# Sixteen pairs in place of twelve in the sum-of-products form of a down projection, and four buffers for its split activations

## The chip, the core and the metric

The kernel runs on one core of a Trainium2 chip. The metric is device time in microseconds of one launch, from all inputs in device memory to the output in device memory. The engines named below are TensorE (PE in the profile; its weight loads are PEld), VectorE (DVE), ScalarE (ACT), GpSimd (POOL) and SyncE (SP, which issues most transfers here). They run their own instruction queues, each in its order, and hand work to each other through semaphores.

## What is computed

The kernel is one decoder layer: token mixers, cross-attention and a gated feed-forward block, for 256 tokens of width 2048. Only the last step of the last block is touched:

```python
def conv_glu_ffn(h, w_up, conv_w, conv_b, w_down):     # h: 256 x 2048
    u = h @ w_up                                       # 256 x 16384
    uc = conv_b + sum(conv_w[j] * shift_right(u, CONV_WIDTH - 1 - j) for j in range(CONV_WIDTH))
    gate, up = split_cols(uc, (D_FF, D_FF))            # D_FF = 8192
    return (jax.nn.gelu(gate, approximate=True) * up) @ w_down   # the down projection: 8192 x 2048

x = x + rms_norm(conv_glu_ffn(h, ffn_w_up, ffn_conv_w, ffn_conv_b, ffn_w_down), ffn_post_norm)
```

All of it is float32. TensorE multiplies rounded operands (float32r), so each operand is split into a rounded part and a rest (hi and lo), and a product is three matmuls: hi by hi, lo by hi, hi by lo.

## The kernel before

**The down projection.** Its output of 256 tokens by 2048 columns is made in two blocks of 1024 columns (`fd`, L2060 to L2063). A block runs over 64 chunks; a chunk is one k tile, 128 rows of `w_down` by 1024 columns, 512 KB. A block holds four PSUM banks (`tm`): token half 0 or 1 by column half 0 or 1, each 128x512. A plain chunk is 4 banks times 3 matmuls, 12 matmuls of 128x512; the activations are the stationary operand, the weights the moving one.

**Feeding a chunk.** SP loads the raw weights (`raw`, four buffers); ACT rounds them into `wh` (five buffers, L448), DVE subtracts for `wl` (L520). When the program stands at chunk i it has written the splits up to chunk i+3 and the loads up to chunk i+7. The activations of two chunks at a time are split by `asplit` (L1911): ACT copies to `as`, DVE subtracts. There are two `as` buffers, and at each even chunk the split for two chunks later is written.

**Pairs.** In each block some neighbouring pairs of chunks, listed in `SEVEN` (L1906), go another way. The pair is a product of 2x2 blocks: the activations as token half by k tile, the weights as k tile by column half (`b11`, `b12` from the first chunk, `b21`, `b22` from the second). It is done with seven block products of sums instead of eight block products, so 7 x 3 = 21 matmuls in place of 24 (`seven_products`, L532). `prepare` (L452) makes the sums in steps, one for each chunk that passes (`ahead_of_pairs`, L492): sums of weights go into `t`, sums of activations into `f` (all inside the tile `end`, which is one buffer for all of them), and their splits into `ts`, `t4` and `sa`. The raw weights of a pair go into the single buffer `sraw`, also in `end`; one of its blocks is overwritten by a sum before it is split. Four of the seven products add up in four further banks (`more`); `join_sums` (L556) adds those together after the last pair of the block, and the evacuation (`fd_evac`) adds the result to the block's own banks.

**What sets the order.** The program order is written by Python loops: `work` (L577) walks over the chunks, and at every chunk calls, in turn, the splits (`lo`), the activations' split, the pair's loads (`pair_loads`, L481), further loads (`dma`), and one step of each pair's preparation that is due. A queue executes in that order, so that an instruction that waits holds all that stand behind it on its engine. Side work such as evacuations is spread by budgets (`Spread`).

Of the kernel before, what the change touches and what calls it, by code (L numbers as in the profile page):

```python
# [10 lines left out]
F32R = mybir.dt.float32r  # L11
# [4 lines left out]
P = 128  # L16
# [138 lines left out]
def _layer(ctx, tc, nc, d, dbg):  # L155
# [12 lines left out]
    def T2(name, shape=None, dt=F32):  # L168
        return mp.tile(shape or [P, 2, S], dt, tag="T2", bufs=6, name=name)
# [221 lines left out]
    class Feed:  # L391
        def __init__(self):
            a, g = blocks[0]["srcs"], blocks[1]["srcs"]
            self.src = a[:LEAD] + [c for p in zip(a[LEAD:], g) for c in p] + g[len(a) - LEAD:]
            self.src += [s for b in blocks[2:] for s in b["srcs"]]
            n, self.pairs, self.preps = sum(len(b["srcs"]) for b in blocks[:2]), {}, []
            for b in blocks[2:]:
                if b["seven"]:
                    for k in b["seven"]["at"]:
                        self.pairs[n + k], self.pairs[n + k + 1] = 0, 1  # L400
                        self.preps.append([n + k - 6, self.prepare(n + k, k), n + k, []])
                n += len(b["srcs"])
            self.raw, self.st, self.nd, self.ns, self.nl, self.nop = {}, {}, 0, 0, 0, 0

        def dma(self, upto):
# [36 lines left out]
        def hi(self, upto):  # L442
            while self.ns <= min(upto, len(self.src) - 1):
                self.dma(self.ns)
                r = self.raw[self.ns]
                wh = self.staged("wh", r)
                for o, v in self.pieces(self.ns, wh, r):
                    nc.scalar.copy(o, v)  # L448
                self.st[self.ns] = [wh, None]
                self.ns += 1  # L450

        def prepare(self, c, k):  # L452

            raw, t, f = M["sraw"], M["sums"], M["f4"]
            (b11, b12), (b21, b22) = ([raw[:, i, j * 512:j * 512 + 512] for j in range(2)] for i in range(2))
            x = acpair(k).rearrange("p k (t s) -> p (k t) s", t=2)
            dve.tensor_add(t[:, 0:512], b22, b12)
            dve.tensor_sub(f[:, 0:2], x[:, 1:2].broadcast_to((P, 2, P)), x[:, 0:4:3])
            yield
            dve.tensor_sub(b12, b12, b11)  # L460
            dve.tensor_sub(f[:, 2], x[:, 0], f[:, 1])
            dve.tensor_sub(f[:, 3], x[:, 2], f[:, 2])
            yield
            dve.tensor_add(t[:, 512:1024], b22, b12)
            sa = [T2("sa", [P, 4, P], F32R) for _ in range(2)]
            M["sa"].append(sa)
            act.copy(sa[0], f)
            yield
            dve.tensor_sub(t[:, 1024:], b21, t[:, 512:1024])
            dve.tensor_sub(sa[1], f, sa[0])  # L470
            ts, t4 = [C("ts", f"bg{j}", [P, 1024], F32R) for j in range(2)], [T2("t4", [P, 512], F32R) for _ in range(2)]
            M["ts"].append((ts, t4))
            act.copy(ts[0], t[:, 0:1024])
            yield
            dve.tensor_sub(ts[1], t[:, 0:1024], ts[0])
            act.copy(t4[0], t[:, 1024:])
            yield
            dve.tensor_sub(t4[1], t[:, 1024:], t4[0])
            yield

# [51 lines left out]
    def seven_products(b, banks, ci, w0h, w0l, w1h, w1l):  # L532
        sv = b["seven"]
        new = "more" not in sv
        if new:
            sv["ready"]()
            sv["more"] = [sv["pool"]("more") for _ in range(4)]
        (t, t4), a, sa = M["ts"].pop(0), M["a4"].pop(0), M["sa"].pop(0)
        half = lambda w, c: [v[:, 0, c * 512:c * 512 + 512] for v in w]
        tops = lambda c: [v[:, c * 512:c * 512 + 512] for v in t]  # L540
        old, more = banks, sv["more"]
        for n, (o, x, w) in enumerate(((more[0], [v[:, 0] for v in a], half((w0h, w0l), 0)),
                                       (old[0], [v[:, 2] for v in a], half((w1h, w1l), 0)),
                                       (more[2], [v[:, 1] for v in sa], half((w0h, w0l), 1)),
                                       (old[1], [v[:, 3] for v in sa], half((w1h, w1l), 1)),
                                       (more[3], [v[:, 0] for v in sa], tops(0)),
                                       (more[1], [v[:, 2] for v in sa], tops(1)),
                                       (old[2], [v[:, 3] for v in a], t4))):
            wh, wl = (turns(v) for v in w)
            mm(o, x[0], wh, start=new and o in more, stop=False)  # L550
            mm(o, x[1], wh, start=False, stop=False)
            mm(o, x[0], wl, start=False, stop=ci == sv["at"][-1] and o in more)
            if n in (1, 3, 5):
                side.half()

    def join_sums(sv):  # L556

        more, s = sv["more"], [M["join"][:, i] for i in range(4)]
        sv["sums"] = s
        act.copy(s[0], more[0])  # L560
        dve.tensor_add(s[2], s[0], more[1])
        yield
        dve.tensor_add(s[1], s[2], more[2])
        dve.tensor_add(s[2], s[2], more[3])
        yield
        dve.tensor_add(s[3], s[1], more[3])
        yield

    def run():
# [1333 lines left out]
        fu = block("fm", W("w_fw", f - 6), fu_xs(f), fw_evac(f), cols=256, wide=lambda k: M["fx"][:, :, k])  # L1903

    M["as"], M["a4"], M["sa"], M["ts"] = {}, [], [], []
    SEVEN = [12, 20, 30, 38, 48, 56], [10, 18, 28, 36, 46, 54]  # L1906

    def acpair(e):
        return M["ac"][e // 16][:, e % 16:e % 16 + 2] if e < 32 else M["ac"][2 + (e - 32) // 8][:, e % 8:e % 8 + 2]
# [1 line left out]
    def asplit(k):  # L1911

        if k not in M["as"]:
            n, e = k // 2, k % 64
            actile(e + 1)
            a = mp.tile([P, 1024], F32R, tag=f"au{n % 2}", bufs=1, name="as")
            a = a.rearrange("p (i j s) -> p i j s", i=2, j=2)
            split(a[:, 0], a[:, 1], acpair(e))
            for j in range(2):
                M["as"][k + j] = (a[:, 0, j], a[:, 1, j])  # L1920
            if e in SEVEN[k // 64]:
                M["a4"].append([a[:, i].rearrange("p k (t s) -> p (k t) s", t=2) for i in range(2)])
        return M["as"][k]
# [36 lines left out]
    def room():  # L1960
        end = mp.tile([P, 2 * KD * S], F32, tag="hT", bufs=1, name="end")
        M["gain"], M["sums"], M["f4"] = end[:, 0:2048], end[:, 2048:3584], end[:, 3584:4096].rearrange("p (k s) -> p k s", k=4)
        M["join"] = end[:, 4096:6144].rearrange("p (i c) -> p i c", i=4)
        M["sraw"] = end[:, 6144:8192].rearrange("p (i c) -> p i c", i=2)

    def load_gain():
# [6 lines left out]
    def fd_evac(n):  # L1973

        def gen(ps):
            if n == 0:
                M["z3", 0] = U("z3", [P, 2, 1024])
            else:
                M["z3", 1] = big("z31", [P, 2, 1024])
            z = M["z3", n]  # L1980

# [78 lines left out]
    fd = []  # L2060
# [106 lines left out]
```

## Time and profile before

| | us |
|---|---|
| median of 3 runs | 1796.6 (1796.27 to 1796.67) |
| the profiled execution | 1796.5 |
| its span, first to last instruction | 1794.7 |
| PE busy | 1785.2 (99%) |
| DVE busy | 1395.6 (78%) |
| ACT busy | 1076.7 (60%) |
| granted clock of TensorE, mean | 0.999 of 2.4 GHz |

The profiled execution lies 0.1 us from the median, and 1.8 us of it are outside of the span. A row of the timeline gives the start of an instruction, its duration, and in brackets the idle time of the engine before it with the instruction that ended it. The duration reaches until the result is written, and the next instruction of the engine may start a little earlier. So what a run of instructions costs an engine is read from start to start.

### The profile page before, as it was taken

The numbers are of one execution on the slowest core, as the hardware profiler recorded it, in microseconds if no ns is written. First come the engines' busy times: TensorE is split into PE (matmuls) and PEld (weight loads), VectorE is DVE, ScalarE is ACT, GpSimd is POOL, SyncE is SP. The second block draws the span as 40 slices with busy tenths as digits, with TensorE's granted clock in tenths as the row PEclk, the third lists the DMA queues.
The fourth block names the chain that finished last, engine by engine and source line by source line (L and its number), as shares of the span: only waits on it lengthen the run. The fifth ranks groups of instructions, "written<-read, shape, count | busy, mean of one in ns | idle before, by whom it ended". The sixth has DMA issues, their size and how long they took to land.

```text
span 1794.7 us, 30098 instructions
## 1 busy us (share of the span) xinstructions
PE 1785.2 (99%) x11778; PEld 1629.7 (91%) x11778; DVE 1395.6 (78%) x2020; ACT 1076.7 (60%) x1616; POOL 28.9 (2%) x51
## 2 busy tenths in 40 slices
PE   9999999999999999999999999999999999999998
PEld 9999988888888999999999999999999998888887
DVE  7869995766665767778878777877777778888887
ACT  7576454654554666677566667666655655556554
POOL 0100000000100000000000000000000000000000
PEclk9999999999999999999999999999999999999999
DMA  8755564454556676656666666666666676767664
GB/s 283 206 170 186 164 190 146 125 180 144 200 188 211 227 243 186 190 150 197 208 203 198 203 209 192 199 206 204 199 200 209 192 229 213 227 186 227 209 209 129
DMA packets 99134, 351.59 MB, mean 196 GB/s; under 512 B 10896, under 2 KB 13968, under 8 KB 98864
## 3 DMA queue, kind: packets, MB, share of 16 engines
q1 hardware_dynamic: 97888, 347.38, 61.3%
q8 instruction: 92, 1.51, 0.3%
q0 software_dynamic: 384, 1.18, 0.2%
q10 hardware_dynamic: 720, 1.12, 0.2%
q14 instruction: 50, 0.41, 0.1%
HBM read 347.01 MB, written 2.10 MB: 195 GB/s over the span
## 4 chain that ended last, share of the span: by engine, by line
PE 99%; DVE 0%; DMA 0%; ACT 0%; issue 0%; SPq 0%; DVEq 0%; ACTq 0%
PE fm L191 55%; PE tm L191 37%; PE more L191 2%; PE gram L191 0%; PE Y L191 0%; PE lv L191 0%; DMA op<-in_op_dram 0%; PE X L191 0%; PE num L191 0%; PE zwa L191 0%; PE U L191 0%; PE gramA L191 0%; PE xo L191 0%; PE zg L191 0%; PE Tn L191 0%; PE mT L1472 0%
## 5 line engine op out<-in xcount | busy, mean ns | idle before, releaser
L520 DVE TENSOR_TENSOR wl<-raw,wh 128x1024 fp32r<-128x1024 f32 (+1 forms) x617 | 741.5, 1218 | 128.6 <-ACT wh L448 125.9
L448 ACT CAST wh<-raw 128x1024 fp32r<-128x1024 f32 (+1 forms) x617 | 633.6, 1044 | 112.7 <-PE tm L191 61.7
L191 PE MATMUL fm<-fx,wh 128*128 128x512 f32 (+1 forms) x2240 | 672.8, 364 | 0.6 <-DVE fx L68 0.4
L191 PE MATMUL fm<-fx,wl 128*128 128x256 f32 x2048 | 558.3, 273 | 0.0
L191 PEld LDWEIGHTS fm<-fx,wh 128*128 128x128 f32 x2240 | 409.3, 190 | 49.9 <-DVE fx L68 1.0
L191 PEld LDWEIGHTS fm<-fx,wl 128*128 128x128 f32 x2048 | 393.3, 192 | 0.0
L191 PE MATMUL tm<-wh,as 128*128 128x512 f32 x856 | 254.8, 379 | 0.0
L191 PE MATMUL tm<-wh,hx 128*128 128x512 f32 (+1 forms) x832 | 243.9, 378 | 1.4 <-ACT hx L68 1.4
L191 PEld LDWEIGHTS tm<-wh,as 128*128 128x128 f32 x856 | 161.7, 189 | 23.2 <-DVE as L68 0.3
L68 ACT COPY ul<-fm 128x256 f32<-128x256 f32 x128 | 44.9, 373 | 225.5 <-PE fm L191 225.5
L191 PE MATMUL fm<-hx,wh 128*128 128x256 f32 x1024 | 174.5, 277 | 0.0
L191 PEld LDWEIGHTS tm<-wh,hx 128*128 128x128 f32 x832 | 151.0, 189 | 21.8 <-POOL wh L507 1.6
L191 PE MATMUL tm<-wl,as 128*128 128x512 f32 x428 | 162.2, 379 | 0.0
L191 PEld LDWEIGHTS fm<-hx,wh 128*128 128x128 f32 x1024 | 155.6, 192 | 1.1
L191 PE MATMUL tm<-wl,hx 128*128 128x512 f32 (+1 forms) x416 | 152.5, 373 | 0.4 <-DVE wl L520 0.3
L68 DVE TENSOR_TENSOR us<-fm,ul 128x256 f32<-128x256 f32 x128 | 48.5, 420 | 131.2 <-ACT ul L68 131.2
L191 PE MATMUL fm<-hx,wl 128*128 128x256 f32 x512 | 140.8, 275 | 0.0
L68 ACT CAST as<-ac 128x512 fp32r<-128x512 f32 x64 | 39.4, 617 | 118.8 <-PE tm L191 118.8
L191 PEld LDWEIGHTS fm<-hx,wl 128*128 128x128 f32 x512 | 98.3, 192 | 0.0
L191 PEld LDWEIGHTS tm<-wl,as 128*128 128x128 f32 x428 | 80.9, 189 | 11.5
L191 PEld LDWEIGHTS tm<-wl,hx 128*128 128x128 f32 x416 | 77.5, 189 | 11.2 <-DVE wl L520 0.5
L191 PE MATMUL fm<-mg,wh 128*128 128x512 f32 (+1 forms) x320 | 84.9, 340 | 0.0
(406 smaller groups left out, 2114.8 us busy)
## 6 DMA issues: line engine op xcount, KB each, us to landing
raw<-in_w_fw_dram SPq DMA_DIRECT2D x232, 512.0 KB, 4.3
raw<-in_w_in_dram SPq DMA_DIRECT2D x160, 512.0 KB, 3.7
raw<-in_w_fd_dram SPq DMA_DIRECT2D x104, 512.0 KB, 4.1
raw<-in_w_br_dram SPq DMA_DIRECT2D x32, 512.0 KB, 4.2
raw<-in_w_mw_dram SPq DMA_DIRECT2D x24, 512.0 KB, 4.8
raw<-in_w_fu_dram SPq DMA_DIRECT2D x24, 512.0 KB, 4.0
end<-in_w_fd_dram SPq DMA_DIRECT2D x24, 512.0 KB, 3.6
raw<-in_w_mo_dram SPq DMA_DIRECT2D x8, 512.0 KB, 4.1
```

What stands on the lines that cost most here:

```text
L68: return f(out, *a, **k)
L191: pe.matmul(out, lhsT, rhs, start=start, stop=stop, skip_group_check=True)
L448: nc.scalar.copy(o, v)
L520: nc.vector.tensor_sub(o, v, h)
```

## The change

- `SEVEN` lists eight pairs in each block where there were six. Most stand six chunks apart (four plain chunks between two pairs); before, the distances were eight and ten.
- `prepare` uses another set of seven products. Its first step makes two sums of weights in one 128x1024 instruction and a third in place of `b11`; it runs in four steps. A preparation starts five chunks ahead of its pair, or, where the pair ahead is six chunks away, as soon as that pair is past, four chunks ahead. Before it started six chunks ahead.
- `seven_products` takes the products in another order and into other banks; `join_sums` adds up accordingly, with one more copy on ACT.
- `asplit` has four buffers: the two of before and the two halves of a new tile `as2`. That tile takes the place in which the first block's result `z3` stood, which goes into `end`; `join` shares its place with the pair's sums, and so the second block's first preparation asks for the first block's evacuation to be written first.

```diff
-                        self.preps.append([n + k - 6, self.prepare(n + k, k), n + k, []])
+                        last = self.preps[-1][2] if self.preps else 0
+                        self.preps.append([max(n + k - 5, last + 2), self.prepare(n + k, k), n + k, []])
...
+            self.second = n - 64 + SEVEN[1][0]
...
+                assert self.pairs.get(self.ns) != 0 or self.ns in self.summed
...
-            raw, t, f = M["sraw"], M["sums"], M["f4"]
-            (b11, b12), (b21, b22) = ([raw[:, i, j * 512:j * 512 + 512] for j in range(2)] for i in range(2))
+            raw, t, f = M["sraw"].rearrange("p i (j n) -> p (i j) n", j=2), M["sums"], M["f4"]
             x = acpair(k).rearrange("p k (t s) -> p (k t) s", t=2)
-            dve.tensor_add(t[:, 0:512], b22, b12)
+            if c == self.second:
+                side.need(fd[0]["task"])
+            dve.tensor_add(t[:, 0:1024].rearrange("p (j n) -> p j n", j=2), raw[:, 0:1].broadcast_to((P, 2, 512)), raw[:, 1:3])
+            dve.tensor_add(raw[:, 0], t[:, 0:512], raw[:, 2])
+            self.summed.add(c)
+            yield
+            dve.tensor_add(t[:, 1024:], raw[:, 0], raw[:, 3])
             dve.tensor_sub(f[:, 0:2], x[:, 1:2].broadcast_to((P, 2, P)), x[:, 0:4:3])
-            yield
-            dve.tensor_sub(b12, b12, b11)
-            dve.tensor_sub(f[:, 2], x[:, 0], f[:, 1])
-            dve.tensor_sub(f[:, 3], x[:, 2], f[:, 2])
-            yield
-            dve.tensor_add(t[:, 512:1024], b22, b12)
-            sa = [T2("sa", [P, 4, P], F32R) for _ in range(2)]
-            M["sa"].append(sa)
-            act.copy(sa[0], f)
-            yield
-            dve.tensor_sub(t[:, 1024:], b21, t[:, 512:1024])
-            dve.tensor_sub(sa[1], f, sa[0])
             ts, t4 = [C("ts", f"bg{j}", [P, 1024], F32R) for j in range(2)], [T2("t4", [P, 512], F32R) for _ in range(2)]
             M["ts"].append((ts, t4))
             act.copy(ts[0], t[:, 0:1024])
             yield
+            dve.tensor_sub(f[:, 2], f[:, 1], x[:, 0])
+            dve.tensor_add(f[:, 3], x[:, 2], f[:, 2])
             dve.tensor_sub(ts[1], t[:, 0:1024], ts[0])
+            sa = [T2("sa", [P, 4, P], F32R) for _ in range(2)]
+            M["sa"].append(sa)
             act.copy(t4[0], t[:, 1024:])
-            yield
+            act.copy(sa[0], f)
+            yield
+            dve.tensor_sub(sa[1], f, sa[0])
             dve.tensor_sub(t4[1], t[:, 1024:], t4[0])
             yield
...
-        for n, (o, x, w) in enumerate(((more[0], [v[:, 0] for v in a], half((w0h, w0l), 0)),
-                                       (old[0], [v[:, 2] for v in a], half((w1h, w1l), 0)),
-                                       (more[2], [v[:, 1] for v in sa], half((w0h, w0l), 1)),
-                                       (old[1], [v[:, 3] for v in sa], half((w1h, w1l), 1)),
-                                       (more[3], [v[:, 0] for v in sa], tops(0)),
-                                       (more[1], [v[:, 2] for v in sa], tops(1)),
-                                       (old[2], [v[:, 3] for v in a], t4))):
+        for n, (o, x, w) in enumerate(((old[1], [v[:, 2] for v in a], half((w1h, w1l), 1)),
+                                       (more[0], [v[:, 0] for v in a], half((w0h, w0l), 1)),
+                                       (old[0], [v[:, 3] for v in sa], half((w1h, w1l), 0)),
+                                       (more[1], [v[:, 2] for v in sa], half((w0h, w0l), 0)),
+                                       (more[2], [v[:, 1] for v in sa], tops(0)),
+                                       (more[3], [v[:, 0] for v in sa], tops(1)),
+                                       (old[3], [v[:, 3] for v in a], t4))):
...
-    SEVEN = [12, 20, 30, 38, 48, 56], [10, 18, 28, 36, 46, 54]
+    SEVEN = [12, 18, 24, 32, 38, 44, 50, 56], [10, 16, 22, 28, 34, 40, 48, 54]
...
-            a = mp.tile([P, 1024], F32R, tag=f"au{n % 2}", bufs=1, name="as")
+            if n == 2:
+                M["as2"] = U("as2", [P, 2, 1024], F32R)
+            a = M["as2"][:, n % 2] if n % 4 > 1 else mp.tile([P, 1024], F32R, tag=f"au{n % 2}", bufs=1, name="as")
...
-        M["join"] = end[:, 4096:6144].rearrange("p (i c) -> p i c", i=4)
+        M["join"] = end[:, 2048:4096].rearrange("p (i c) -> p i c", i=4)
+        M["z3", 0] = end[:, 4096:6144].rearrange("p (t c) -> p t c", t=2)
```

On VectorE, around the second pair of the first block (`end` holds the raw weights of the pair and its sums; `wl<-end` are the splits of the pair's own weights), the queue before reads:

```order
L68 TENSOR_TENSOR end<-end 128x512
L68 TENSOR_TENSOR end<-ac 128x256
L520 TENSOR_TENSOR wl<-raw,wh 128x1024
L68 TENSOR_TENSOR end<-end 128x512
L68 TENSOR_TENSOR end<-ac,end 128x128 x2
L68 TENSOR_TENSOR as<-ac,as 128x512
L520 TENSOR_TENSOR wl<-raw,wh 128x1024
L68 TENSOR_TENSOR end<-end 128x512
L520 TENSOR_TENSOR wl<-end,wh 128x1024
L68 TENSOR_TENSOR end<-end 128x512
L68 TENSOR_TENSOR sa<-end,sa 128x512
```

and now, at the second pair of the first block, from the preparation's first instruction to `sa`:

```order
L68 TENSOR_TENSOR end<-end 128x1024
L68 TENSOR_TENSOR end<-end 128x512
L522 TENSOR_TENSOR wl<-end,wh 128x1024
L68 TENSOR_TENSOR end<-end 128x512
L68 TENSOR_TENSOR end<-ac 128x256
L68 TENSOR_TENSOR as<-ac,as 128x512
L522 TENSOR_TENSOR wl<-end,wh 128x1024
L68 TENSOR_TENSOR end<-end,ac 128x128
L68 TENSOR_TENSOR end<-ac,end 128x128
L68 TENSOR_TENSOR ts<-end,ts 128x1024
L522 TENSOR_TENSOR wl<-raw,wh 128x1024
L68 TENSOR_TENSOR sa<-end,sa 128x512
```

The split of the pair's first chunk, `wl<-end`, now stands directly behind the sum that is written in place of its raw block, and `sa` stands one chunk later against the pair. On ScalarE, the same places before:

```order
L448 CAST wh<-raw 128x1024
L68 CAST sa<-end 128x512
L448 CAST wh<-end 128x1024
L68 CAST ts<-end 128x1024
L68 CAST as<-ac 128x512
L448 CAST wh<-end 128x1024
```

and now:

```order
L451 CAST wh<-raw 128x1024
L451 CAST wh<-end 128x1024
L68 CAST ts<-end 128x1024
L68 CAST as<-ac 128x512
L451 CAST wh<-end 128x1024
L68 CAST t_16110<-end 128x512
L68 CAST sa<-end 128x512
L451 CAST wh<-raw 128x1024
```

The copy `sa` moved from ahead of the pair's weights to behind both of them, directly ahead of the next chunk's `wh`. On PE, the first pair's products before, three matmuls each:

```order
L191 MATMUL more<-wh,as 128x512 x2
L191 MATMUL more<-wl,as 128x512
L191 MATMUL tm<-wh,as 128x512 x2
L191 MATMUL tm<-wl,as 128x512
L191 MATMUL more<-wh,sa 128x512 x2
L191 MATMUL more<-wl,sa 128x512
L191 MATMUL tm<-wh,sa 128x512 x2
L191 MATMUL tm<-wl,sa 128x512
```

and now:

```order
L191 MATMUL tm<-wh,as_15831 128x512 x2
L191 MATMUL tm<-wl,as_15831 128x512
L191 MATMUL more<-wh,as_15831 128x512 x2
L191 MATMUL more<-wl,as_15831 128x512
L191 MATMUL tm<-wh,sa 128x512 x2
L191 MATMUL tm<-wl,sa 128x512
L191 MATMUL more<-wh,sa 128x512 x2
L191 MATMUL more<-wl,sa 128x512
```

`sa` is still first used by the third product, its second part `sa[1]` by that product's second matmul, the eighth of the pair. Over the whole program PE has 11100 matmuls where it had 11112; nothing but the down projection differs in its queue.

## Rows read from the trace of the kernel before

**Rows 1.** The page's first part: busy time of each engine, its share, instructions.

```profile
PE 1785.2 (99%) x11778; PEld 1629.7 (91%) x11778; DVE 1395.6 (78%) x2020; ACT 1076.7 (60%) x1616; POOL 28.9 (2%) x51
```

**Rows 2.** Windows: stretch, length, busy PE, PEld, DVE, ACT, POOL, PEclk, DMA, GB/s.

```profile
8.00:12.00 4.00, 3.62 (x23) 2.90 (x23) 4.00 (x10) 3.72 (x9) 0.43 (x1) 1.00 1.00 402
1470.00:1625.00 155.00, 155.00 (x719) 135.73 (x719) 129.78 (x157) 90.58 (x112) 0.00 (x0) 1.00 0.69 219
```

**Rows 3.** Timeline of PE (start, duration, instruction) close to its end.

```profile
1779.74 0.59 PE L191 MATMUL tm<-wh,as 128*128 128x512 f32 x2
...
1786.22 0.59 PE L191 MATMUL tm<-wh,as 128*128 128x512 f32 x2
```

**Rows 4.** Waits in the down projection: who, for whom, us in total, times, longest.

```profile
ACT as L68 <- PE tm L191: 118.8, 61, 2.7
...
PEld tm L191 <- DVE as L68: 0.3, 1, 0.3
```

**Rows 5.** The tile `tm`: matmuls with `sa`, durations in ns, first and last start.

```profile
L191 PE MATMUL tm<-wh,sa x24: 379/379/380, 1495.9 to 1763.6; 128*128 128x512 f32 x24
```

**Rows 6.** Timeline of DVE: the first pair's `sa`, then the second pair's preparation.

```profile
1488.93 0.68 DVE L68 TENSOR_TENSOR sa<-end,sa 128x512 fp32r<-128x512 f32 x1
...
1501.48 0.68 DVE L68 TENSOR_TENSOR end<-end 128x512 f32<-128x512 f32 x1
1502.08 0.42 DVE L68 TENSOR_TENSOR end<-ac 128x256 f32<-128x256 f32 x1
1502.41 1.22 DVE L520 TENSOR_TENSOR wl<-raw,wh 128x1024 fp32r<-128x1024 f32 x1
1503.55 0.69 DVE L68 TENSOR_TENSOR end<-end 128x512 f32<-128x512 f32 x1
1504.15 0.61 DVE L68 TENSOR_TENSOR end<-ac,end 128x128 f32<-128x128 f32 x2
1504.68 0.69 DVE L68 TENSOR_TENSOR as<-ac,as 128x512 fp32r<-128x512 f32 x1
...
1506.66 0.68 DVE L68 TENSOR_TENSOR end<-end 128x512 f32<-128x512 f32 x1
...
1509.80 0.69 DVE L68 TENSOR_TENSOR as<-ac,as 128x512 fp32r<-128x512 f32 x1
```

**Rows 7.** Timeline of ACT in the same stretch.

```profile
1505.39 0.61 ACT L68 CAST sa<-end 128x512 fp32r<-128x512 f32 x1
1505.91 1.05 ACT L448 CAST wh<-end 128x1024 fp32r<-128x1024 f32 x1
1507.37 1.05 ACT L68 CAST ts<-end 128x1024 fp32r<-128x1024 f32 x1 [0.41 <-DVE end L68]
...
1509.15 0.62 ACT L68 CAST as<-ac 128x512 fp32r<-128x512 f32 x1 [0.73 <-PE tm L191]
```

**Rows 8.** Timeline of DVE: last multiply of the first block's evacuation, next preparation's start.

```profile
1634.23 0.68 DVE L68 TENSOR_TENSOR z<-end 128x512 f32<-128x512 f32 x1
...
1638.16 0.68 DVE L68 TENSOR_TENSOR end<-end 128x512 f32<-128x512 f32 x1
```

**Rows 9.** DMA issues of the down projection: KB each, us to landing; then the raw tiles.

```profile
raw<-in_w_fd_dram SPq DMA_DIRECT2D x98, 512.0 KB, 4.1
end<-in_fpg_dram SPq DMA_DIRECT2D x1, 1024.0 KB, 6.7
...
DMA to landing us min/median/max: 3.4/4.1/7.5
```

**Rows 10.** Timeline of PE in the first microseconds, with two of its waits.

```profile
7.76 0.95 PE L191 MATMUL tm<-wh,hx 128*128 128x296 f32 x4 [1.38 <-ACT hx L68]
...
9.15 0.67 PE L191 MATMUL tm<-wh,hx 128*128 128x296 f32 x4
9.65 0.43 PE L191 MATMUL tm<-wl,hx 128*128 128x296 f32 x2
...
11.05 0.52 PE L191 MATMUL tm<-wl,hx 128*128 128x296 f32 x2 [0.29 <-DVE wl L520]
```

More of the change, by code (lines that the diff above doesn't have):

```diff
@@ L395, in __init__ @@
             self.src += [s for b in blocks[2:] for s in b["srcs"]]
-            n, self.pairs, self.preps = sum(len(b["srcs"]) for b in blocks[:2]), {}, []
+            n, self.pairs, self.preps, self.summed = sum(len(b["srcs"]) for b in blocks[:2]), {}, [], set()
             for b in blocks[2:]:
@@ L559, in join_sums @@
         sv["sums"] = s
-        act.copy(s[0], more[0])
-        dve.tensor_add(s[2], s[0], more[1])
+        act.copy(s[1], more[0])
+        dve.tensor_add(s[3], s[1], more[1])
         yield
-        dve.tensor_add(s[1], s[2], more[2])
-        dve.tensor_add(s[2], s[2], more[3])
+        act.copy(s[0], more[2])
+        dve.tensor_sub(s[0], s[0], s[3])
+        dve.tensor_sub(s[3], s[3], more[3])
         yield
-        dve.tensor_add(s[3], s[1], more[3])
+        dve.tensor_add(s[2], s[0], more[3])
         yield
@@ L1975, in gen @@
         def gen(ps):
-            if n == 0:
-                M["z3", 0] = U("z3", [P, 2, 1024])
-            else:
+            if n:
                 M["z3", 1] = big("z31", [P, 2, 1024])
```

## Prediction

> **What bounds the kernel now.** The page's first part comes first: PE is busy 99% of the span, DVE 78%, ACT 60% [rows 1]. An average hides stages, so the window over the middle of the down projection is next: from 1470 to 1625 us PE is busy for all of 155.00 us at a granted clock of 1.00, DVE for 129.78, ACT for 90.58 [rows 2]. PE sets the end there. What it pays for one 128x512 matmul is read from start to start: from 1779.74 to 1786.22 lie 30 matmuls [rows 3], 6.48 / 30 = 0.216 us. So a chunk (12) is 2.59 us, a pair (21) 4.53, and two pairs six chunks apart (21 and four chunks, 69 matmuls) are 14.90 us apart. The waits say how far the feeders are ahead: the only long one is ACT's for a free `as` buffer, 118.8 us in 61 times; PE waits once, 0.3 us, when the stage begins [rows 4]. `sa` of the first pair is written from 1488.93 [rows 6], first used at 1495.9 [rows 5]: over 6 us early.
>
> **What goes.** Four pairs more, at 3 matmuls: 12 x 0.216 = **-2.59 us**, all on the path, since nothing else ends last.
>
> **What it asks of VectorE.** The question is whether DVE can prepare a pair in 14.90 us, since the preparations now follow each other at that distance. Costs from start to start [rows 6]: 128x1024 takes 1502.41 to 1503.55, 1.14; 128x512 takes 1503.55 to 1504.15, 0.60; 128x256 takes 0.33; the two 128x128, the second of which reads the first, 0.53. Six chunks with one preparation have eight of 128x1024 (six `wl`, the double sum, `ts`), seven of 128x512 (two sums, `sa`, `t4`, three `as`), the 128x256 and the two 128x128: 9.12 + 4.20 + 0.33 + 0.53 = 14.18. That fits, with 0.72 to spare. But the order of the queue adds waits that no spare time takes up, because DVE and ACT wait for each other in turn:
> - The second sum reads the first, just written. An instruction that waits starts 0.03 after the one it waits for has ended: DVE's sum ends 1506.66 + 0.68 = 1507.34 and ACT starts 1507.37; ACT's `as` ends 1509.77 and DVE starts 1509.80 [rows 6, 7]. So 1.22 + 0.03 in place of 1.14: 0.11.
> - `wl` of the pair's first chunk stands directly behind the sum written in place of the raw block; ACT rounds that block first, and `wl` waits for ACT: 0.68 + 0.03 + 1.05 + 0.03 = 1.79 from the sum's start where 0.60 would do: 1.19. Behind it on DVE stand the other sums, all `wl` that follow, and `sa`.
> - `sa` on ACT waits for the last 128x128 and stands ahead of the next chunk's `wh`, for which DVE's next `wl` waits, and that stands ahead of `sa`'s second part. From that 128x128's start: 0.29 + 0.03 (the two lasted 0.61, twice 0.29 and the 0.03 between), the copy 0.52 (1505.39 to 1505.91 [rows 7]), `wh` 1.05 + 0.03, together 1.92; DVE's own work is 0.20 (0.53 less 0.32) and 1.14 (`ts`), so 0.58.
>
> With these 1.88 us DVE's round is **16.06 us against PE's 14.90**: at each further six-chunk distance the preparation falls 1.16 us back. What is late next is `sa`'s second part, which the pair's eighth matmul needs.
>
> **How much lead there is.** At the second pair of a run of six-chunk distances, count from the first pair's first matmul. The last plain chunk ahead of the second pair takes its `wh` buffer when the eighth matmul lets go of one, 7 x 0.216 + 0.38 [rows 5] + 0.03 = 1.92; `wh` ends at 2.97, its `wl` starts at 3.00, the double sum at 4.14, the second sum at 5.39, `wl` of the pair at 7.18, then 1.14, 0.60, 0.33, 0.60 and 1.14 to the 128x128 at 10.99, its second at 11.32, the next chunk's `wl` 1.92 later at 13.24, `sa` at 14.38, ready at 15.09. PE needs it at 14.90 + 1.51 = 16.41: 1.32 us of lead, where there were over 6. Distances of eight chunks (93 matmuls, 20.09 us) restore it.
>
> **Where PE then waits.** First block: 12, 18, 24 uses 1.32 and then 0.16, no wait. 32, 38, 44, 50, 56: no wait at 38 and 44, 1.00 at 50, 1.16 at 56. Second block: 10, 16, 22, 28, 34, 40: none at 16 and 22, 1.00 at 28, 1.16 at 34 and at 40. 48 to 54: none. Sum **+5.48 us**. PE's waits are the price in full, since nothing behind them makes up time on an engine without gaps.
>
> **Smaller terms.** The gain vector, 1024 KB, lands 6.7 us after its issue, and raw tiles behind it may land as late as 7.5 where the median is 4.1 [rows 9]. ACT was held by the `as` buffers and never met a late tile; with four buffers it is, in front of the long run of the first block. That can cost nothing (a late tile can't gain), or all of that run's lead and as much again, 2.5 us; I take **+0.6**, nearer to nothing, since four raw buffers, 4 x 2.59 = 10.4 us, stand between a load and its use. After a wait PE's first matmuls are slower: a group that took 0.43 took 0.52 behind a short wait, and one of 0.67 took 0.95 behind 1.38 us [rows 10], so 0.1 to 0.28 in each of two runs (of the stalls inside a run it comes out of the next one's): **+0.3**. At nothing I put: the evacuation that is asked for ahead of the second block's first preparation (its last multiply starts at 1634.23, 3.9 us ahead of the preparation at 1638.16 [rows 8], which now starts a chunk later); one more copy on ACT in `join_sums`, 0.6 us under ACT's idle 40%, with the last chunks' matmuls as cover; the new tile `as2`, whose first use has nothing to wait for; ACT's shorter waits, which are the lead and no time of PE's.
>
> **Sum.** -2.59 + 5.48 + 0.6 + 0.3 = +3.8. The profiled execution is 1796.5, 0.1 below the median, its span 1794.7 with 1.8 outside that don't change: 1796.5 + 3.8 = **1800.3 us**.
>
> **Rivals.**
> *VectorE keeps pace.* DVE's 84% in the window speaks for it, and 14.18 is under 14.90. It needs the three waits to be hidden, by reordering that the queues don't do; then only the products count: 1793.9, faster. Chance 0.09. That the change saves no matmuls is excluded by the queue's count, 11100 against 11112.
> *A wait for the result costs nothing beyond the queue's own pace.* The two 128x128 of which the second reads the first take 0.53, and I read 0.13 of it (0.53 less twice 0.20) as the wait for the result; if instructions of VectorE never start before the one ahead is out, that 0.13 and the first wait of 0.11 are no loss against my 14.18. Against it stands that 1.14 from start to start, for an instruction that lasts 1.22 [rows 6], lets the next one start before the result is out. Without 0.24 the round is 15.82, the loss 0.92, the lead 1.56; then waits of 0.28 and 0.92 in the first block, of 0.28 + 0.92 + 0.92 in the second, 3.32 in all: -2.59 + 3.32 + 0.6 + 0.3 = +1.6, 1798.1, not slower. Chance 0.08. The Trainium skill ("VectorE: DVE Perf Modes", section "The DRAIN you can't avoid") has this as a rule: the next instruction doesn't start until the pipe is empty, and a semaphore behind each of eight copies cost nothing extra. The trace doesn't agree: 1.14 is less than 1.22.
> *The lead is less than I count.* A raw tile that is late, or a wait at the run's first pair, takes the 1.32 us away in some runs: each such run pays up to 1.32 us more, three to four runs 4 to 5 us: 1802 to 1805. The raw loads of 4.1 us on the median speak against, 7.5 for it [rows 9]. Chance 0.16.
> *Every six-chunk distance pays.* If lateness of loads feeds itself (a late `wl` frees a raw buffer late, and the load behind it lands late), the lead never comes back: 12 x 1.16 = 13.9, so 1796.5 - 2.6 + 13.9 + 0.3 = 1808.1, slower. It decides from loads that land later than the 10.4 us of the four buffers; the longest landed in 7.5 [rows 9]. Chance 0.06.
> *The clock falls.* The waits are micro-pauses on a matmul engine that ran without one. At half the clock a pair is 4.53 us longer; were it so for the five pairs that wait, 22.7 us more: 1823. Behind a wait of 1.38 us the profile still has a granted clock of 1.00 for the window [rows 2, 10], so 0.03. The Trainium skill ("TensorE: Matmul & The Clock Gate", section "A second HAM failure mode: psum-queue depth-cycling") tells of a clock that swings when short pauses recur between groups of matmuls; the row at hand doesn't show it, with pauses of another cause.
>
> **How the numbers follow.** The forecast has 0.58, and its own range is 1798.8 (no lateness, no restart, waits 10% smaller) to 1802.0 (2.5 for the gain's load in place of 0.6). What a measurement of this kernel can tell from no change is 0.2%, 3.6 us: slower begins at 1800.2. So the forecast is halved by it. Faster, under 1793.0, has the low edge of the first rival: 0.02. Within: 0.07 and 0.08 of the first two rivals, and 0.27 of the forecast: 0.42. Slower: 0.31 of the forecast, 0.16, 0.06, 0.03: 0.56. The range leaves the first rival out below and the last two above, with some of the lost lead's: 1797.5 to 1804.5.
>
> **What would show it.** In the timeline of PE, waits of about 1 us for DVE's `sa` at the eighth matmul of the pairs 50 and 56 of the first block and 28, 34 and 40 of the second, and of no others; 12 matmuls fewer. In DVE's, the `wl` behind the second sum starts 1.8 us after it, and from one `sa` to the next at six chunks 16.1 us. ACT's waits for `as` buffers gone. Wrong I am if PE waits nowhere (first rival), if it waits for `wl` or raw tiles rather than `sa`, or if the granted clock of the stage leaves 1.00.

## The result and the profile after

| | before | after |
|---|---|---|
| median, us | 1796.59 (1796.16 to 1797.93, 12 executions) | 1800.71 (1800.17 to 1802.19, 12 executions) |
| profiled execution, us | 1796.5 | 1801.5 |
| its span, us | 1794.7 | 1799.3 |

The changed kernel is slower by 4.1 us: the ratio is 1.0023, 95% interval 1.0015 to 1.0031. The forecast was 1800.3. Not all of the 4.1 lies in the span: on the median 1.78 us of an execution of before lie outside of its span (from the executions of before beside the experiments), and 2.14 of one of after. So 0.36 us come ahead of the first instruction or behind the last, and about 3.8 lie between them.

The page's first part of after, and then the window over the middle of its down projection (columns as in [rows 1, 2]):

```profile
PE 1784.9 (99%) x11766; PEld 1627.3 (90%) x11766; DVE 1412.9 (79%) x2044; ACT 1085.3 (60%) x1630; POOL 28.6 (2%) x51
```

```profile
1470.00:1625.00 155.00, 152.57 (x704) 132.46 (x703) 137.50 (x168) 94.83 (x119) 0.00 (x0) 1.00 0.65 216
```

On the page PE has 12 matmuls fewer, and in a window in which it had no gap it now has 2.43 us of them. VectorE is busier, and still far from full: the shares say nothing of the cause. The granted clock stays 1.00. The waits of the stage, in the columns of [rows 4], name what is late:

```profile
DVE wl L522 <- ACT wh L451: 29.1, 35, 2.3
...
ACT sa L68 <- DVE end L68: 24.2, 16, 1.6
...
PEld tm L191 <- DVE sa L68: 8.2, 8, 1.4
...
PE tm L191 <- DVE sa L68: 5.3, 6, 1.0
```

ACT's 118.8 us for free `as` buffers are gone; in their place VectorE and ScalarE wait for each other, and PE waits for `sa`. These are all of PE's waits in the timeline of the two blocks' matmuls; the pairs are 24, 50 and 56 of the first block, 28, 34 and 40 of the second:

```profile
1526.16 0.48 PE L191 MATMUL tm<-wh,sa 128*128 128x512 f32 x1 [0.52 <-DVE sa L68]
1526.48 0.38 PE L191 MATMUL tm<-wl,sa 128*128 128x512 f32 x1
...
1592.27 0.48 PE L191 MATMUL tm<-wh,sa 128*128 128x512 f32 x1 [0.96 <-DVE sa L68]
...
1608.39 0.48 PE L191 MATMUL tm<-wh,sa 128*128 128x512 f32 x1 [0.96 <-DVE sa L68]
...
1700.39 0.48 PE L191 MATMUL tm<-wh,sa 128*128 128x512 f32 x1 [0.97 <-DVE sa L68]
...
1716.51 0.48 PE L191 MATMUL tm<-wh,sa 128*128 128x512 f32 x1 [0.96 <-DVE sa L68]
...
1732.62 0.48 PE L191 MATMUL tm<-wh,sa 128*128 128x512 f32 x1 [0.95 <-DVE sa L68]
```

The bracket shows 0.96, the price is more, since the idle time counts from the modelled end of the matmul ahead. From start to start 1592.27 to 1608.39 is 16.12 us where 69 matmuls take 14.90: **1.22 us each**, in which is the slower restart (from 1526.16 to 1526.48 is 0.32 where 0.216 is usual). Pair 24 costs 0.78, pairs 22 and 44 a restart of 0.1 each. Five times 1.22 and 0.78 and 0.2, less 2.59 for the twelve matmuls, is +4.5; the spans differ by 4.6. Why 16.12 is seen in VectorE's timeline, one round from `sa` to `sa`:

```profile
1575.41 0.68 DVE L68 TENSOR_TENSOR sa<-end,sa 128x512 fp32r<-128x512 f32 x1
...
1581.22 1.94 DVE L68 TENSOR_TENSOR end<-end 128x1024 f32<-128x1024 f32 x2
1584.33 1.23 DVE L522 TENSOR_TENSOR wl<-end,wh 128x1024 fp32r<-128x1024 f32 x1 [1.16 <-ACT wh L451]
...
1588.15 0.28 DVE L68 TENSOR_TENSOR end<-end,ac 128x128 f32<-128x128 f32 x1
1588.47 0.29 DVE L68 TENSOR_TENSOR end<-ac,end 128x128 f32<-128x128 f32 x1
1588.68 1.22 DVE L68 TENSOR_TENSOR ts<-end,ts 128x1024 fp32r<-128x1024 f32 x1
1590.39 1.23 DVE L522 TENSOR_TENSOR wl<-raw,wh 128x1024 fp32r<-128x1024 f32 x1 [0.50 <-ACT wh L451]
1591.53 0.68 DVE L68 TENSOR_TENSOR sa<-end,sa 128x512 fp32r<-128x512 f32 x1
```

There are the two waits for ScalarE that the prediction named, 1.16 and 0.50. ScalarE's side of the first is the rounding at 1583.24, which starts as the in-place sum is written (the bracket names no releaser for it). Its side of the second: behind the copy at 1586.61 it has nothing to do until the last 128x128 is done, and `sa` stands ahead of the `wh` that VectorE wants:

```profile
1583.24 1.05 ACT L451 CAST wh<-end 128x1024 fp32r<-128x1024 f32 x1 [5.13 <-issue]
...
1586.61 0.61 ACT L68 CAST t<-end 128x512 fp32r<-128x512 f32 x1
1588.79 0.62 ACT L68 CAST sa<-end 128x512 fp32r<-128x512 f32 x1 [1.56 <-DVE end L68]
1589.32 1.04 ACT L451 CAST wh<-raw 128x1024 fp32r<-128x1024 f32 x1
```

### The profile page after: what moved, and what is told of

The parts are those of the page before. It is cut to its first block, busy times and chain, and to the rows that moved or that the text cites. A ratio compares the mean times of both kernels' runs of the same rounds, so it can differ in the third digit from the quotient of the medians.

```text
span 1799.3 us, 30167 instructions
## 1 busy us (share of the span) xinstructions
PE 1784.9 (99%) x11766; PEld 1627.3 (90%) x11766; DVE 1412.9 (79%) x2044; ACT 1085.3 (60%) x1630; POOL 28.6 (2%) x51
## 4 chain that ended last, share of the span: by engine, by line
PE 96%; DVE 1%; ACT 1%; DMA 1%; issue 1%; POOL 0%; DVEq 0%; ACTq 0%; POOLq 0%
PE fm L191 54%; PE tm L191 35%; PE more L191 2%; ACT wh L451 0%; PE gram L191 0%; DMA op<-in_op_dram 0%; PE Y L191 0%; PE lv L191 0%; PE X L191 0%; DVE wl L522 0%; PE num L191 0%; PE zwa L191 0%; PE U L191 0%; PE gramA L191 0%; DVE sa L68 0%
## 5 line engine op out<-in xcount | busy, mean ns | idle before, releaser
L522 DVE TENSOR_TENSOR wl<-raw,wh 128x1024 fp32r<-128x1024 f32 (+1 forms) x609 | 731.9, 1218 | 131.8 <-ACT wh L451 129.5
L451 ACT CAST wh<-raw 128x1024 fp32r<-128x1024 f32 (+1 forms) x609 | 627.2, 1044 | 146.3 <-PE tm L191 82.2
L191 PE MATMUL tm<-wh,as 128*128 128x512 f32 x800 | 237.9, 379 | 0.0
L191 PEld LDWEIGHTS tm<-wh,as 128*128 128x128 f32 x800 | 151.1, 189 | 21.4
L191 PE MATMUL tm<-wl,as 128*128 128x512 f32 x400 | 151.6, 379 | 0.0
L191 PEld LDWEIGHTS tm<-wl,as 128*128 128x128 f32 x400 | 75.6, 189 | 10.7
L191 PE MATMUL fm<-mg,wl 128*128 128x256 f32 x256 | 69.9, 273 | 0.0
```

What stands on the lines that cost most here:

```text
L191: pe.matmul(out, lhsT, rhs, start=start, stop=stop, skip_group_check=True)
L522: nc.vector.tensor_sub(o, v, h)
```

## The experiments

**Theory:** VectorE's round at six chunks is 16.12 us against 14.90 by the order of two queues, and PE waits where a lead of about 1.2 us is used up. **Rivals:** VectorE's amount of work, the loads, or the new preparation and its buffers as such. Every kernel below is the kernel after with one edit, or two where that is said. A "series" is a row of pairs at six chunks from each other; the prediction calls it a run. "Lead" is the time from the end of the write of `sa`'s second part to the matmul that reads it (0.06 where PE waits for it).

**Only the table.** As many pairs, at most two six-chunk distances in a row.

```diff
-    SEVEN = [12, 18, 24, 32, 38, 44, 50, 56], [10, 16, 22, 28, 34, 40, 48, 54]
+    SEVEN = [12, 18, 24, 32, 38, 44, 52, 58], [10, 16, 22, 30, 36, 42, 50, 56]
```

> Only the table of pairs differs from the kernel after: still eight pairs in each block and the same preparation, but never more than three pairs six chunks apart in a row, except three with the last two ([12, 18, 24, 32, 38, 44, 52, 58] and [10, 16, 22, 30, 36, 42, 50, 56]). Theory (VectorE's round of 16.12 us against PE's 14.90 uses up a lead of 1.2 us that eight chunks restore): the second six-chunk distance of a run just uses the lead up, so PE waits about 0.7 us at pair 24 of the first block, under 0.3 at pairs 44, 22 and 42, and nowhere else; 1796.6 - 2.6 + about 1 = 1795.0 us (1794.3 to 1796). Rival (every six-chunk distance costs PE, or the new products and buffers cost by themselves): 9 such distances of 12 stay, so about 1799 to 1801.

Measured: 1794.74 us, 0.9988 of before (0.9979 to 0.9997). The leads are 1.26 at the second pair of each series, 0.06 at the third, 3.7 behind each eight-chunk distance; the five waits are gone with ten of the twelve six-chunk distances still there (ten, not the nine of the expectation). This is the third pair of the first series, where the lead is just used up (`sa` written at 1524.78 + 0.69 = 1525.47):

```profile
1524.78 0.69 DVE L68 TENSOR_TENSOR sa<-end,sa 128x512 fp32r<-128x512 f32 x1
```

```profile
1525.28 0.72 PE L191 MATMUL tm<-wh,sa 128*128 128x512 f32 x2
1525.84 0.38 PE L191 MATMUL tm<-wl,sa 128*128 128x512 f32 x1
```

What costs is the length of the series, not the single distance. Pair 24 paid only a restart here (0.1, where 0.7 had been expected). Against after 6.0 us are had back without one instruction less.

**The queue's order: three kernels.** The first makes the sums that need nothing from ScalarE before VectorE gets to the wait of 1.16:

```diff
             self.summed.add(c)
-            yield
             dve.tensor_add(t[:, 1024:], raw[:, 0], raw[:, 3])
             dve.tensor_sub(f[:, 0:2], x[:, 1:2].broadcast_to((P, 2, P)), x[:, 0:4:3])
+            yield
```

> The kernel after, but two instructions of the preparation that need nothing from ScalarE (the third sum of weights, 128x512, and the first of the activations, 128x256) stand ahead of the weight split of the pair's first chunk, in the time in which VectorE waits for ScalarE. Simple theory: 0.60 + 0.33 of the 1.16 us wait are filled, the round is 16.12 - 0.93 = 15.19. By the hand-overs in full, less: the split of the pair's second chunk then meets ScalarE, whose rounding of the two chunks, of the sums and of the activations (0.95 + 0.95 + 0.52 + 1.05) ends 4.21 us after the in-place sum's start, where VectorE gets there at 4.46 now; so only 0.25 us is won, the round is 15.87, the loss 0.97. PE waits about 0.2 at pair 24, 0.5 and 1.0 at 50 and 56, 0.5, 1.0 and 1.0 at 28, 34 and 40: 4.1 us, 1798.1 us (1797.5 to 1798.8). Simple theory: 1794 to 1795. Rival that these waits are not the cause: 1800.7.

Measured: 1798.38 us, ratio 1.0009 (1.0000 to 1.0018). The round is 15.86 (1713.39 to 1729.25 between the eighth matmuls of pairs 34 and 40), as the expectation's second theory had it; the waits stand at 50 and 56, 28, 34 and 40, and pair 24 has a lead of 0.54. The wait of 1.16 went, and most came back at once:

```profile
1705.72 1.23 DVE L522 TENSOR_TENSOR wl<-end,wh 128x1024 fp32r<-128x1024 f32 x1
1707.18 0.69 DVE L68 TENSOR_TENSOR as<-ac,as 128x512 fp32r<-128x512 f32 x1 [0.23 <-ACT as L68]
1708.12 1.23 DVE L522 TENSOR_TENSOR wl<-end,wh 128x1024 fp32r<-128x1024 f32 x1 [0.26 <-ACT wh L451]
```

VectorE now runs into ScalarE at the pair's second chunk. Two engines that feed each other in turn have one chain, and only its longest way counts.

The second kernel makes the dependent 128x128 sums one step earlier:

```diff
             dve.tensor_sub(f[:, 0:2], x[:, 1:2].broadcast_to((P, 2, P)), x[:, 0:4:3])
+            dve.tensor_sub(f[:, 2], f[:, 1], x[:, 0])
+            dve.tensor_add(f[:, 3], x[:, 2], f[:, 2])
...
-            dve.tensor_sub(f[:, 2], f[:, 1], x[:, 0])
-            dve.tensor_add(f[:, 3], x[:, 2], f[:, 2])
```

> The kernel after, but the two dependent 128x128 activation sums are made one step earlier, beside the 128x256 one, so that ScalarE's copy sa has no wait for them when its turn comes. Theory: the 0.5 to 0.58 us that VectorE waits for the next chunk's rounding behind that copy go, nothing else comes in their place (ScalarE would be done 1.07 us ahead), the round is 15.54, the loss 0.64 and the lead 1.8: no wait at 24 and 50, 0.1 at 56, none at 28, 0.1 at 34 and 0.64 at 40; 1796.6 - 2.6 + 0.9 = 1794.9 us (1794.3 to 1795.8). Rival (this wait only hides another, of loads or of VectorE's own work): 1799 to 1800.7.

Measured: 1796.40 us, ratio 0.9998 (0.9990 to 1.0007); the expectation missed by 1.5. The wait of 0.50 is gone, but the round is 15.66, not 15.54: the 128x128 sums now stand right behind the 128x256 whose result they read, and that costs a wait too, 0.45 from start to start where 0.33 was.

```profile
1706.10 0.42 DVE L68 TENSOR_TENSOR end<-ac 128x256 f32<-128x256 f32 x1
1706.55 0.29 DVE L68 TENSOR_TENSOR end<-end,ac 128x128 f32<-128x128 f32 x1
```

In [rows 6] the same 128x256 is followed by work that doesn't need it, 0.33 later. With a loss of 0.76 the leads are 1.73, 0.96, 0.19, and then PE waits: at 56, 34 and 40, three waits of 0.7 to 0.8, 2.2 us in all where 0.9 had been worked out.

The third kernel has both edits.

> Both moves: all sums of a pair that need nothing from ScalarE stand ahead of the weight split of the pair's first chunk. Theory: from the in-place sum, VectorE's splits of the pair's two chunks start at 2.06 and 4.21 us and that of the next chunk at 6.49, where it was 7.85; the round is 14.76 us, less than PE's 14.90, so no pair waits and only the products count: 1796.6 - 2.6 = 1794.0 us (1793.6 to 1794.6). VectorE's amount of work is the same as in the kernel after. Rival (VectorE's amount of work at six chunks, or the loads, set the pace): 1797 to 1800.7.

Measured: 1794.26 us, ratio 0.9988 (0.9979 to 0.9997). PE has no wait for `sa` any more: the lead at every six-chunk distance is 2.63 or 2.64 and stays. VectorE does the same work, and in the window it is busier than in after:

```profile
1470.00:1625.00 155.00, 155.00 (x720) 135.73 (x719) 142.25 (x173) 97.64 (x121) 0.00 (x0) 1.00 0.68 228
```

So 142.25 of 155 us are no bound where 137.50 went with waits: VectorE's amount of work is ruled out, and so are the loads: in this trace too ScalarE waits 2.09 us for a raw tile at 1479.34, and PE does not. The median is 2.5 us below that of before, where the twelve matmuls promise 2.59.

**The old table.** The new preparation, products and buffers at the distances of before.

```diff
-    SEVEN = [12, 18, 24, 32, 38, 44, 50, 56], [10, 16, 22, 28, 34, 40, 48, 54]
+    SEVEN = [12, 20, 30, 38, 48, 56], [10, 18, 28, 36, 46, 54]
```

> The kernel after with the table of the kernel before (twelve pairs, eight and ten chunks apart): new preparation, new products, four buffers. Theory (the new preparation costs PE nothing by itself, only the six-chunk distances do): no wait of PE for sa, as many matmuls as before, 1796.6 us (1796.2 to 1797.1). Rival (the later sa, the added copy in the join or the buffers' place cost by themselves): 1797.5 to 1800.

Measured: 1796.49 us, ratio 0.9997 (0.9988 to 1.0006), no wait of PE, leads of 4.5 to 5.0 at each pair. Taken together, the new preparation, the join's added copy and the buffers' new places cost nothing that shows.

**Two activation buffers.** The table and the preparation of after stay.

```diff
-            if n == 2:
-                M["as2"] = U("as2", [P, 2, 1024], F32R)
-            a = M["as2"][:, n % 2] if n % 4 > 1 else mp.tile([P, 1024], F32R, tag=f"au{n % 2}", bufs=1, name="as")
+            a = mp.tile([P, 1024], F32R, tag=f"au{n % 2}", bufs=1, name="as")
```

> The kernel after with the two activation buffers of before; the table and the preparation stay. Theory (the 1.2 us lead is what the four buffers give, since ScalarE's copy to a buffer in use waits for PE, and VectorE's work for the next pair then starts later against PE): no lead at any pair, so that all twelve six-chunk distances cost PE at least the 1.22 us that five cost now, more if the round grows by the wait for the buffer: 1796.6 - 2.6 + 12 x 1.22 = 1808.6 us or more, up to 1820. Rival (the buffers are not what the time hangs on): 1800.7.

Measured: 1823.79 us, ratio 1.0148 (1.0133 to 1.0164): slower than the floor of 1808.6 by far, and above the range. The waits of its down projection:

```profile
ACT as L68 <- PE tm L191: 79.3, 32, 4.6
...
PEld tm L191 <- DVE sa L68: 28.1, 12, 2.4
...
PE tm L191 <- DVE sa L68: 23.3, 12, 2.0
```

All twelve six-chunk distances pay, 2.2 us each (17.12 between the eighth matmuls of pairs 44 and 50), because the round now holds ScalarE's wait for PE as well, which is handed on to VectorE:

```profile
1588.59 0.62 ACT L68 CAST as<-ac 128x512 fp32r<-128x512 f32 x1 [2.88 <-PE tm L191]
```

```profile
1589.24 0.69 DVE L68 TENSOR_TENSOR as<-ac,as 128x512 fp32r<-128x512 f32 x1 [0.61 <-ACT as L68]
1590.18 1.23 DVE L522 TENSOR_TENSOR wl<-raw,wh 128x1024 fp32r<-128x1024 f32 x1 [0.25 <-ACT wh L451]
```

VectorE had neither wait at this place in after. The twelve cost some 26.5 us; 3.4 more come from the clock, and they are told of in the last section. So this table needs the four buffers: at the distances of before they and all the rest bring nothing (e5_old_table), with this table they are worth 23 us. What two buffers would cost in the better order of e4_both was not run.

**Why pair 24 waits.** The prediction put 0.6 us on the gain vector's load. In after, ScalarE waits for late raw tiles at the start of the block, and in the gain's place:

```profile
1476.75 1.05 ACT L451 CAST wh<-raw 128x1024 fp32r<-128x1024 f32 x1 [1.73 <-DMA raw<-in_w_fd_dram]
1480.26 1.04 ACT L451 CAST wh<-raw 128x1024 fp32r<-128x1024 f32 x1 [2.46 <-DMA raw<-in_w_fd_dram]
1529.68 1.04 ACT L451 CAST wh<-raw 128x1024 fp32r<-128x1024 f32 x1 [1.56 <-DMA raw<-in_w_fd_dram]
1533.45 1.04 ACT L451 CAST wh<-raw 128x1024 fp32r<-128x1024 f32 x1 [2.20 <-DMA raw<-in_w_fd_dram]
```

The lead at pair 18 is 0.60, at pair 38 it is 1.26, as in the second block where no gain is loaded. That points to the waits at the block's start. A first attempt issued the loads of each pair behind a wider distance three chunks later:

```diff
-                    if i >= max(c - 12, before + c - p[2]):
+                    if i >= max(c - 9, before + c - p[2]):
```

> The kernel after, but the two loads of a pair that follows a wider distance, the block's first pair above all, are issued three chunks later (up to nine chunks ahead in place of twelve). In the profiled execution of after, ScalarE waited 1.73 and 2.46 us for raw tiles at 1476.75 and 1480.26, behind these loads, and PE waited at pair 24. Theory (loads at the start of the block take the lead of the first run in some executions): ScalarE meets no late raw tile between 1470 and 1482, the lead at pair 18 is 1.26 and PE does not wait by more than 0.1 at pair 24; 1800.2 us, and the executions lie closer together than after's 1800.2 to 1802.2. Rival (the gain vector's load at chunk 24 made that wait, as the prediction had it): pair 24 waits as before, 1800.7.

Measured: 1801.90 us (1801.67 to 1802.24), ratio 1.0028 (1.0017 to 1.0039). The late tiles at the start and the wait at pair 24 are gone (lead 1.26 at 18), but the edit met pair 32 too: its `sa` comes 1.3 later, the lead at pair 38 is 0.07, pair 44 waits, and there are six waits of 1.22. The expected 1800.2 is wrong for a reason that bears the theory out: who takes 1.2 us of lead from a series gets them back as PE's wait. Then for the first pair alone (`c - (9 if p is self.preps[0] else 12)`), together with the unchanged kernel after and one with the gain vector at chunk 58 (`if kk == 58:`):

> The kernel after, but only the loads of the first block's first pair are issued three chunks later; the pair after a wider distance (32) keeps its own, which in the run before this lost the second run's lead (0.07 at pair 38 in place of 1.26, one more wait of 1.22). Theory: no late raw tile at the start of the block, lead 1.26 at pair 18 and at pair 38, no wait over 0.1 at pair 24, five waits of 1.22: 1796.7 - 2.59 + 6.1 + 0.2 = 1800.4 us (1800.1 to 1800.7), the executions within 0.6 us of each other. Rival (the lead of the first run has another cause): as after in the same rounds, and as scattered.

> The kernel after unchanged, on the same chip. Theory: most executions near 1800.4 with five waits of 1.22 us, those above it by 0.5 to 1 us with a further wait at pair 24 behind a raw tile that came late at the start of the block; median 1800.4 to 1800.9. Rival: if all lie at 1801.2 or above, pair 24 always waits.

> The kernel after with the gain vector's load at chunk 58 of the first block, behind its last pair, in place of chunk 24. The prediction put +0.6 us on this load, by the lead of the run from pair 32 on. Theory now: ScalarE's waits for raw tiles at 1528 to 1534 us go, the lead at pair 38 stays 1.26, as it was in after with the load in place, and the time stays that of after to 0.3 us. Rival (the prediction's): the lead at pair 38 grows and 0.3 to 1 us is won.

Measured: 1800.94 us (1800.26 to 1801.56), 1800.88 (1800.69 to 1801.36) and 1800.59; ratios 1.0023, 1.0025 and 1.0022. With later first loads the trace has a lead of 1.26 at 18 and five waits; one raw tile is still late (1.13 us at 1481.13), which had not been expected. In after itself the lead at 18 is 0.99 this time, with a wait of 0.4 at pair 24, where the first trace had 0.60 and 0.78. With the gain vector later, the lead is 1.26 at 18 and 1.26 at 38, as it is at 38 with the gain in its place, so the gain takes nothing from the series behind it. ScalarE's waits at the two late tiles of the block's start, in after itself and then with the gain later (1.73 and 2.46 in the first trace of after):

```profile
1476.77 1.04 ACT L451 CAST wh<-raw 128x1024 fp32r<-128x1024 f32 x1 [1.48 <-DMA raw<-in_w_fd_dram]
1480.15 1.04 ACT L451 CAST wh<-raw 128x1024 fp32r<-128x1024 f32 x1 [2.33 <-DMA raw<-in_w_fd_dram]
```

```profile
1476.23 1.05 ACT L451 CAST wh<-raw 128x1024 fp32r<-128x1024 f32 x1 [1.18 <-DMA raw<-in_w_fd_dram]
1479.17 1.04 ACT L451 CAST wh<-raw 128x1024 fp32r<-128x1024 f32 x1 [1.89 <-DMA raw<-in_w_fd_dram]
...
1528.48 1.05 ACT L451 CAST wh<-raw 128x1024 fp32r<-128x1024 f32 x1 [0.98 <-DMA raw<-in_w_fd_dram]
```

The later these two tiles, the smaller the lead: 2.96, 3.34 and 4.07 at pair 12 in the three traces with the first loads in their place, 4.58 in both traces with later first loads. So the wait at pair 24 (0.78 and 0.4 in the two traces of after) goes with late raw tiles at the block's start; the trace with the gain later, whose first loads are those of after, shows that it can also stay away without an edit of the loads. In the time none of this is seen: the medians of the spans are 1798.8, 1798.7 and 1798.8 us, and the executions with later first loads lie 1.3 us apart where 0.6 was expected, and those of after in the same rounds 0.7. That the kernel with the gain later is 0.3 lower in the median lies outside of the span (1.79 us there, 2.14 in the other two). What makes the tiles late, and what makes the time outside of the span differ, was not settled.

**More pairs.** Both order edits, and nine pairs in each block, all six apart:

```diff
+    SEVEN = [10, 16, 22, 28, 34, 40, 46, 52, 58], [8, 14, 20, 26, 32, 38, 44, 50, 56]
```

> As e4_both (both moves), with nine pairs in each block, all six chunks apart ([10, 16, ..., 58] and [8, 14, ..., 56]). Theory (a round of VectorE that PE's 14.90 us covers may be repeated without end): no wait of PE, 2 x 3 matmuls fewer than e4_both, 1794.26 - 1.30 = 1793.0 us (1792.5 to 1793.5). Rival (without an eight-chunk distance some lateness piles up, in the loads or in ScalarE): 1795 to 1798.

Measured: 1792.61 us (1792.10 to 1793.58), ratio 0.9977 of before (0.9967 to 0.9986), faster than both kernels. PE has no wait for `sa`; in the first block the lead is 1.82 at the second pair and grows to 2.63, at 14.75 per round against PE's 14.89, and stays there.

## Why the prediction was right

- **Matmuls.** 12 x 0.216 = 2.59: right. With the waits away, 2.5 us are won (e4_both).
- **VectorE's round.** 16.06 forecast, 16.12 measured. Nearly all of the 0.06 lies in the hand-over of the in-place sum: ScalarE starts 0.08 behind its end (1581.22 + 1.94 to 1583.24), not 0.03.
- **Lead.** 1.32 forecast, 1.26 measured in three series of four, of which the last 0.06 can't be used. In before it was 5.9 by the measure used here (1489.61 to 1495.51), not over 6: `sa` first enters a product that goes into `more`, ahead of the row of `tm` that was read. Nothing rests on it.
- **Waits.** The places are as forecast, five of five; the sizes were 1.00 or 1.16 and are 1.22 all, since the lead of 1.26 is gone after one more distance, with nothing left over. 5.48 and 0.3 of restarts were forecast, 6.1 (restarts in it) and 0.2 measured.
- **The gain vector, +0.6: the step that failed.** It costs nothing. A term of that size exists in the first series, at pair 24, and not in all traces. The late tiles were foreseen, the place wasn't: behind the gain's load stands an eight-chunk distance, and the lead at pair 32 is 3.71 with the load there and 3.69 without. The four raw buffers, 10.4 us by the prediction, did not keep ScalarE from waiting up to 2.46 us for a tile.
- **Outside of the span.** 1.8 us "that don't change" were assumed; they became 2.14, and why stays open.
- **The number.** That 1800.3 came within 0.4 of 1800.7 is in part luck: the waits and restarts were sized some 0.5 too small, the gain's 0.6 that isn't there made up for it, and the 0.36 outside of the span was in no term. The places and the cause of the waits were right without luck.
- **Zero terms.** Evacuation, join and `as2`: e5_old_table shows them at nothing, taken together.
- **The rivals.** *VectorE keeps pace* needs two moves in the queue, and is then true (e4_both). *A wait for the result costs nothing* is refuted by the rows 1588.15 to 1588.68 above: the second 128x128 starts 0.04 behind the end of the first, whose result it reads, and `ts`, which reads nothing new, 0.21 behind the second's start, 0.08 ahead of its end. The Trainium skill ("VectorE: DVE Perf Modes", section "The DRAIN you can't avoid") has the next instruction start when the pipe is empty, but says in the same paragraph, which the prediction left out, that one that is not held starts earlier. The start of `ts` agrees with the second half and not with the first. *The lead is less than I count* came true in the first series of after alone, by 0.66 and 0.27 of 1.26 in the two traces, at 0.78 and 0.4 us. *Every distance pays* is what two buffers would do, at 2.2 us; lateness of loads that feeds itself is not seen in after, where the lead is back at 3.7 behind each eight-chunk distance. *The clock falls* did not happen in after, and did behind two of twelve waits that were twice as long.

## What to carry to other kernels

Where a second engine prepares for PE, work out its round from start to start with each hand-over, not its busy share, and hold it against PE's distance; a small deficit costs nothing until the lead is used up, and then costs in full at each repetition. Two engines that wait for each other in turn are mended by independent work in the gap of both, and one move alone may only shift the wait. A wider distance now and then is as good as a shorter round, if the lead is that small.

## What the runs showed of the hardware

In the kernel with two buffers PE waited twelve times for 1.90 to 1.96 us, and behind two of these waits the granted clock fell to the lower of its two levels, 1.2 GHz, for about 3.4 us each, by windows of 5.50, 3.20 and 3.50 us with a mean of 0.98, 0.50 and 0.51 (columns as in [rows 2]); the waits in the timeline are at 1512.14 and 1699.60.

```profile
1508.00:1513.50 5.50, 3.60 (x17) 2.81 (x16) 4.96 (x9) 3.98 (x5) 0.00 (x0) 0.98 0.77 285
1513.50:1516.70 3.20, 3.20 (x9) 2.53 (x8) 2.06 (x2) 0.00 (x0) 0.00 (x0) 0.50 0.61 200
1516.70:1520.00 3.30, 3.30 (x17) 2.86 (x16) 1.89 (x3) 1.57 (x2) 0.00 (x0) 1.00 0.63 236
...
1701.00:1704.50 3.50, 3.50 (x10) 2.74 (x9) 2.01 (x2) 0.00 (x0) 0.00 (x0) 0.51 0.67 233
```

In each fall eight matmuls took 0.427 us from start to start in place of 0.216, so each cost 1.7 us. Behind the other ten waits there is no fall, and behind the waits of 0.96 in after there is none either; why those two, no run shows.

That PE's pauses between groups can make the clock swing is what the Trainium skill tells ("TensorE: Matmul & The Clock Gate", section "A second HAM failure mode: psum-queue depth-cycling"). Here it is seen behind two pauses of 1.9 us out of twelve, and not lastingly; in the prediction it had been priced at five pairs and 22.7 us.
